# A two-head-group block on one core: latents' small rows inside the context's gate products, context decays behind the first scores, a head's end in the next head's stage

## The chip, the core and the metric

The kernel runs on one core of a Trainium2 chip. Five engines work side by side, each through its own list of instructions in order: PE (TensorE, matrix products; PEld is its weight load), DVE (VectorE, elementwise work and scans), ACT (ScalarE, functions and copies), POOL (GpSimd) and SP (SyncE, which here issues most DMAs). The metric is the time of one execution on the device in microseconds (us), the median over runs. The profile also shows the share of its clock that TensorE was granted, called PEclk or clock here.

## The reference

One layer of a hybrid block, for 512 latent tokens and 256 context tokens of width 2048. The two streams are normalised and modulated, projected with one weight matrix, run through four heads of gated linear attention (GLA) and four heads of mLSTM in both directions, gated, projected, and followed by a feed-forward block with a 3x3 convolution. What the change touches is the GLA and the gates of both groups:

```python
z = jnp.einsum('btd,dp->btp', h, w_in)
gq, gk, gv, gg, glr, mq, mk, mv, mo, mgate = jnp.split(z, PROJ_SPLITS, axis=-1)
dec = jnp.einsum('btr,zrk->zbtk', glr, gla_w_lr) + gla_b_lr[:, None, None, :]
gla_loga = jax.nn.log_sigmoid(dec) / GLA_NORMALIZER
# per chunk: S_t = diag(a_t) S_{t-1} + k_t v_t^T ; o_t = S_t^T q_t
# y_gla = rmsnorm(o) * silu(gate);   y_ml = sigmoid(ogate) * rmsnorm(h)
pre = mgate + mlstm_b_gate                    # input and forget gates of the mLSTM
```

`glr` (16 columns) and `mgate` (16 columns) are the small rows: they are needed before any decay or gate. The context is scanned first, and its last state starts the scan of the latents.

## The kernel before

All products are made from split operands (a high and a low part), three products for one, so that a block of 128 x 512 weights (`raw_h`, 512 KB) is loaded by DMA, its high part cast on ACT (`hi_h`), its low part subtracted on DVE (`lo_h`), and then used in 36 kinds of products named `a`.

The projection of one head (`project_steps`) takes 8 such blocks (`kp` 0 to 7), each in six steps (`a_0` to `a_5`). `weave` lays the chain of one head (a generator, its stage) into the projection of the next: the stage yields a number, and that many microseconds of projection products, by a table of costs, are put on PE before the stage goes on. On PE the written order is kept; on the other engines a list scheduler sets it. So the numbers that are yielded decide how much PE work covers each step's wait for ACT and DVE.

- Before the first stage, the small rows of latents and context are made as products `gm` (L592 to L598), with 32 columns each, four at a time; ACT copies them (`gm` copy), a product with a constant sums the four groups (`glr`, in `small_rows`, L601), ACT casts, DVE subtracts the low part.
- The first stage (`first_stages`) holds GLA heads 0 and 1, whose projections are done by then, and covers them with head 2's projection. `gla_prep` (L662) makes the decays of a head: `wlr` from a small weight (ACT cast L667, DVE L668), products `dec` for both directions, log-sigmoid (Abs, Exp, Ln on ACT, L641 to L643, then DVE L644), the context's products `cdec` and their log-sigmoid `cla`, the scans `bt` (L690), the context's sums `csum` and `kd` (L701).
- `gla` makes seven levels of scores: per level DVE subtracts decays twice (`ex`, L94), ACT takes two exponentials, DVE multiplies by q and k (L97), PE makes four products `sl`, DVE writes them under a mask (L762). Between them lie the states: `cst`, the transposes `ktt`, the products `st` with their update on DVE (L807), and at the end the outputs `po`. `finish` normalises a head (`ob`, L653), transposes it on PE (`yt`) and copies it (`yT`).
- The stage of head 3 ends with `ml_gates`: products `pre`, their bias on DVE (L842), a log-sigmoid, four scans, then transposes `pa` and products `pgc`. `mlstm` is the stage of each mLSTM head; its outputs `po` come in pairs of directions, with a reciprocal `dn` on DVE after each.
- `fill` works off fillers, one chunk of the modulation weights each (`raw_m`, 512 KB by DMA, one DVE operation of L320), at `rate` per weight block.

PE has two PSUM banks (`psb`) for all these small results, used in turn: a product waits until the result before last has been read.

Of the kernel before, what the change touches and what calls it, by code (L numbers as in the profile page):

```python
# [11 lines left out]
F32 = mybir.dt.float32  # L12
# [15 lines left out]
H = 4  # L28
# [55 lines left out]
def block_kernel(ctx: ExitStack, tc: tile.TileContext, a: dict, out: bass.AP):  # L84
# [318 lines left out]

    def project_first():

        banks = [acc(f"a0_{g}", BANKS[g]) for g in range(6)]
        both = accp.tile([P, CJ, T], F32, name="e0_c", tag="sums")
        sums = [None] * 4 + [both[:, j, 0 : DK + DV] for j in range(CJ)]
# [160 lines left out]
    nc.sync.dma_start(wsm, a["w_small"])  # L569
    cr = [tmp.tile([KT, P], F32, name=f"cr{i}", tag="rows") for i in range(2)]  # L570
# [15 lines left out]
    gm = [ytile(i, f"gm{i}", (P, n)) for i, n in enumerate((T, TC))]  # L586
    pinned[0] = True
    for c0, n, hs, m in ((0, T, hx, gm[0]), (T, TC, hc, gm[1])):
        ps = psb(f"gm{c0}", (P, n))
        for k in range(KT):  # L590
            g = 32 * (k % 4)
            parts = [h[k].bitcast(F32) for h in hs]  # L592
            if hs is hx and not 4 <= k < 8:
                parts = [xl[k]]
            for i, part in enumerate(parts):
                mm(ps[g : g + 32, :], wsm[:, k, :], part, start=(k < 4 and i == 0),
                   stop=(k >= 12 and i == len(parts) - 1), skip_group_check=True)
        S.copy(m, ps)  # L598
    st_0.close()

    def small_rows():  # L601
        for c0, n, m in ((0, T, gm[0]), (T, TC, gm[1])):
            ps = psb(f"glr{c0}", (96, n))
            mm(ps, cc(C_SA, 96), m, start=True, stop=True)
            o = glr[0:96, c0 : c0 + n]
            S.copy(o, ps)
            V.scalar_tensor_tensor(out=o, in0=o.bitcast(F32), scalar=cc(C_LO, 1, 96), in1=ps, op0=ALU.mult, op1=ALU.add)
            yield 1.4

# [52 lines left out]
    def gla_prep(h, out):  # L662

        raw = wtile(f"wlraw{h}", "wlraw", 2, DK)[0:98]
        nc.sync.dma_start(raw, a["w_lr"][h])
        wlr = wk.tile([98, 2, DK], F32R, name=f"wlr{h}", tag="wlr")
        S.copy(wlr, raw)  # L667
        V.scalar_tensor_tensor(out=wlr, in0=wlr.bitcast(F32), scalar=cc(C_LO + 1, 1, 98), in1=raw,  # L668
                               op0=ALU.mult, op1=ALU.add)
        la = wtile(f"la{h}", "la", 2, T)  # L670
        t = wtile(f"lt{h}", "tmp", 2, T)
        cla = wtile(f"cla{h}", "cla", CJ, 2, DK)
        ct = ytile(15, f"ct{h}", (P, CJ, 2, DK))
        for d in range(2):
            ps = psb(f"dec{h}{d}")
            mm(ps, wlr[:, d, :], glr[:, 0:T], start=True, stop=True)
            log_sigmoid(la[:, d], ps, t[:, d])
            yield
        ps = psb(f"cdec{h}", (P, CJ, 2, DK))
# [5 lines left out]
        bt = [ytile(8 + d, f"bt{h}{d}") for d in range(2)]  # L685
        for d in range(2):
            o, x = bt[d], la[:, d]
            if d == 1:
                o, x = o[:, ::-1], x[:, ::-1]
            V.tensor_tensor_scan(out=o, data0=cc(C_SEG, T), data1=x, initial=0.0, op0=ALU.mult, op1=ALU.add)  # L690
# [9 lines left out]
        kd = ytile(14, f"kd{h}", (P, 2, CJ, DK))  # L700
        S.activation(kd, ps, AF.Exp, scale=DECAY)  # L701
        ends = wtile(f"ends{h}", "ends", 2, 2, TJ - 1)
        for d in range(2):
            at = P * d + (P - 1) * (1 - d)
            V.tensor_scalar(out=ends[:, 0, d, :], in0=bt[d][:, at : at + 2 * P + 1 : P], scalar1=DECAY, scalar2=None,
                            op0=ALU.mult)
        S.activation(ends[:, 1], ends[:, 0], AF.Exp)
        out.update(bt=bt, kd=kd, ends=ends)
        yield

# [26 lines left out]
    def gla(h, pair, qk, v, kn, vn, yT, prep, fill, after, pending):  # L737
        bt, kd, ends = (prep[n] for n in ("bt", "kd", "ends"))
# [11 lines left out]
        yield fill[0]  # L750
        for lv, b in enumerate(LEVELS):
# [10 lines left out]
            V.copy_predicated(scd, msk[:, lv, :].unsqueeze(1).to_broadcast([P, TJ, P]), ps)  # L762
# [5 lines left out]
            if lv == 1:  # L768

                for j in range(CJ):  # L770
                    mul(kd[:, :, j], kd[:, :, j], kn[j].unsqueeze(1).to_broadcast([P, 2, DK]))
# [53 lines left out]
    def ml_gates():  # L825
# [11 lines left out]
        for t, r in ((0, li), (1, pf)):  # L837
            for c0, n, at in ((0, T, lat0), (T, TC, ctx0)):
# [5 lines left out]
                yield 1.4  # L844
        log_sigmoid(pf, pf, ab)
# [13 lines left out]
        yield 13  # L859
# [32 lines left out]
    def mlstm(h, _, qk, v, kn, vn, yT):  # L892
# [64 lines left out]
        for j in range(TJ):  # L957
            for d in range(2):
# [24 lines left out]
    def first_stages(tiles):  # L983

        yield from small_rows()
        prep = gla_prep(0, preps[0])
        for need in (0, 3, 3, 2.5):
            next(prep)
            yield need
        gla_ahead(0, preps[0])  # L990
        end = yield from gla(0, *tiles, yT, preps[0], (2, 1), gla_prep(1, preps[1]), lambda: None)
# [7 lines left out]
        gla_ahead(2, preps[2])  # L999

    def stages(h, tiles):

        yield 2.7
        if h >= H:
            yield from mlstm(h, *tiles, yT)
        elif h + 1 < H:
            end = yield from gla(h, *tiles, yT, preps[h], (4, 1.8), gla_prep(h + 1, preps[h + 1]), lambda: None)
            yield 5
            end()
            gla_ahead(h + 1, preps[h + 1])  # L1010
        else:
# [453 lines left out]
```

## Time and profile before

| | us |
|---|---|
| median of 3 runs | 2473.45 (2472.29 to 2475.78) |
| the profiled execution | 2479.69 |
| its span from first to last instruction | 2478.0 |
| PE busy | 2418.5 (98%) |
| DVE busy | 1792.9 (72%) |
| ACT busy | 1004.7 (41%) |
| mean granted clock | 0.992 |

The profiled execution is 6.24 us above the median; differences are taken within it. PE's share of busy time is high because the projections and the feed-forward part fill most of the span; the stages that the change touches lie between 197 us and 720 us, and what is lost there is seen only in a view of that stretch: PE's idle time, and the windows in which the granted clock is 0.50.

### The profile page before, as it was taken

To read this page: it belongs to the slowest core of one execution; us is meant where nothing else is said; L and a number is where in the kernel's file an instruction comes from. 1 tells how busy PE (TensorE), PEld (TensorE's weight loads), DVE (VectorE), ACT (ScalarE), POOL (GpSimd) and SP (SyncE) were. 2 spreads that over 40 slices of the span, in tenths; PEclk is the share of its full clock that TensorE was granted. 3 is DMA by queue.
4 is the path that set the end of the run, shared out by engine and by line. 5 is a ranking of instruction groups with operands and counts; after the bars stand their busy time and mean duration, and the time that the engine had idled before them with its cause. 6 is when DMAs were issued, how large, how long until landed. Compare 5 with 4: busy or idle time off the path is not lost.

```text
span 2478.0 us, 38665 instructions
## 1 busy us (share of the span) xinstructions
PE 2418.5 (98%) x15412; PEld 2179.5 (88%) x15412; DVE 1792.9 (72%) x2876; ACT 1004.7 (41%) x1494; POOL 177.4 (7%) x221
## 2 busy tenths in 40 slices
PE   6999989999999999999999999999999999999998
PEld 4887888889888888888999999999999999999997
DVE  6665855644457676669988787878687878787886
ACT  4224433222223232237544444444444444444445
POOL 0000000000000000000111111111101010101021
PEclk9999999999999999999999999999999999999999
DMA  9751111123345878853365555555546464646464
GB/s 383 277 178 49 45 43 43 61 82 113 128 163 190 265 269 306 271 184 115 97 168 125 148 123 147 124 144 124 141 120 152 120 152 117 156 115 158 119 181 135
DMA packets 122388, 373.65 MB, mean 151 GB/s; under 512 B 13912, under 2 KB 18912, under 8 KB 122208
## 3 DMA queue, kind: packets, MB, share of 16 engines
q1 hardware_dynamic: 95200, 318.75, 39.4%
q0 software_dynamic: 25920, 51.40, 11.5%
q8 instruction: 120, 1.97, 0.3%
q10 hardware_dynamic: 1088, 1.05, 0.1%
q14 instruction: 60, 0.49, 0.1%
HBM read 320.80 MB, written 50.34 MB: 150 GB/s over the span
## 4 chain that ended last, share of the span: by engine, by line
PE 81%; issue 10%; DVE 6%; DMA 1%; ACT 1%; POOL 1%; SPq 0%; DVEq 0%; POOLq 0%; ACTq 0%
PE a L111 18%; PE uv L111 16%; PE dn L111 15%; PE ug L111 15%; PE ga L111 7%; PE wo L111 3%; PE ps_m L111 2%; PE po L111 1%; PE sl L111 1%; DVE cv L1232 1%; DMA raw_uv<-in_w_up 1%; PE st L111 1%; PE cst L111 1%; DVE lo_d L106 0%; DVE ex L94 0%
## 5 line engine op out<-in xcount | busy, mean ns | idle before, releaser
L111 PE MATMUL dn<-gh,lo_d 128*128 128x512 f32 x672 | 263.0, 391 | 2.5 <-DVE lo_d L106 2.3
L111 PE MATMUL dn<-gh,hi_d 128*128 128x512 f32 x672 | 262.3, 390 | 0.0
L111 PE MATMUL dn<-gl,hi_d 128*128 128x512 f32 x672 | 262.1, 390 | 0.0
L1232 DVE SCALAR_TENSOR_TENSOR cv<-pads,cwt,cv 128x512 f32<-128x512 f32 x344 | 239.1, 746 | 0.6
L1286 POOL DMA_DIRECT2D x2d<-st x160 | 140.2, 932 | 1147.2 <-ACT st L1285 1069.0
L106 DVE TENSOR_TENSOR lo_buv<-sum_uv,hi_buv 128x1024 fp32r<-128x1024 f32 x80 | 98.0, 1225 | 102.5 <-ACT hi_buv L105 102.5
L320 DVE SCALAR_TENSOR_TENSOR raw_m<-raw_m,crow 128x1024 f32<-128x1024 f32 x128 | 152.8, 1219 | 2.6 <-DMA raw_m<-in_w_mod 2.6
L111 PEld LDWEIGHTS dn<-gh,lo_d 128*128 128x128 f32 x672 | 126.5, 188 | 31.4 <-DVE lo_d L106 5.3
L111 PE MATMUL a<-hi_h,hTh 128*128 128x256 f32 x512 | 149.7, 292 | 0.5 <-ACT e L402 0.5
L111 PEld LDWEIGHTS dn<-gl,hi_d 128*128 128x128 f32 x672 | 126.6, 188 | 26.1
L111 PEld LDWEIGHTS dn<-gh,hi_d 128*128 128x128 f32 x672 | 126.6, 188 | 25.8
L111 PE MATMUL a<-lo_h,hTh 128*128 128x256 f32 x512 | 145.3, 284 | 0.0
L111 PE MATMUL a<-hi_h,hTl 128*128 128x256 f32 x512 | 145.1, 283 | 0.0
L105 ACT CAST hi_d<-raw_d 128x1024 fp32r<-128x1024 f32 x86 | 88.7, 1031 | 131.6 <-PE ug L111 70.6
L106 DVE TENSOR_TENSOR lo_d<-raw_d,hi_d 128x1024 fp32r<-128x1024 f32 x86 | 102.9, 1196 | 48.8 <-ACT hi_d L105 48.1
L111 PE MATMUL ug<-bth,hi_bug 128*128 128x256 f32 x480 | 136.8, 285 | 0.1
L111 PE MATMUL uv<-bth,lo_buv 128*128 128x256 f32 x480 | 135.9, 283 | 0.8 <-DVE lo_buv L106 0.8
L111 PE MATMUL uv<-bqh,lo_auv 128*128 128x256 f32 x480 | 135.9, 283 | 0.0
L111 PE MATMUL uv<-bth,hi_buv 128*128 128x256 f32 x480 | 135.9, 283 | 0.0
L111 PE MATMUL ug<-bqh,lo_aug 128*128 128x256 f32 x480 | 135.8, 283 | 0.0
L111 PE MATMUL uv<-btl,hi_buv 128*128 128x256 f32 x480 | 135.8, 283 | 0.0
L111 PE MATMUL ug<-bqh,hi_aug 128*128 128x256 f32 x480 | 135.8, 283 | 0.0
(408 smaller groups left out, 7270.8 us busy)
## 6 DMA issues: line engine op xcount, KB each, us to landing
raw_m<-in_w_mod SPq DMA_DIRECT2D x192, 512.0 KB, 5.2
raw_d<-in_w_down SPq DMA_DIRECT2D x82, 512.0 KB, 3.5
raw_ug<-in_w_up SPq DMA_DIRECT2D x80, 512.0 KB, 3.5
x2d<-st POOLq DMA_DIRECT2D x160, 256.0 KB, 5.4
raw_uv<-in_w_up SPq DMA_DIRECT2D x80, 512.0 KB, 6.6
raw_h<-in_w_heads SPq DMA_DIRECT2D x64, 512.0 KB, 3.6
raw_ga<-in_w_gates SPq DMA_DIRECT2D x32, 512.0 KB, 4.2
raw_wo<-in_w_out SPq DMA_DIRECT2D x32, 512.0 KB, 4.4
```

The costliest lines, as they stand in the source:

```text
L105: cast[0] = S.copy(hi, x).ins
L106: return V.tensor_tensor(out=lo, in0=x, in1=hi.bitcast(F32), op=ALU.subtract).ins
L111: ins = PE.matmul(*args, **kw)
L320: V.scalar_tensor_tensor(out=x, in0=x, scalar=1.0, in1=crow[0], op0=ALU.mult, op1=ALU.mult, accum_out=mtot[:, at : at + 1])
L1232: V.scalar_tensor_tensor(out=t3, in0=src, scalar=w, in1=t3, op0=ALU.mult, op1=ALU.add)
L1286: nc.gpsimd.dma_start(x2d[k], t, accum_op=ALU.add)
```

## The change

1. The latents' `glr` product, with its copy and subtraction, is put behind the eighth k-tile of the context's `gm` products; the context's is put into the first stage, behind the second `dec`. The `gm` copies get high priority.
2. Head 0's small decay weight is loaded early into a spare part of another tile (`early_w`), ahead of the first stage.
3. In `gla_prep` of head 0 the scans come right behind the two `dec`, and the context's `cdec`, `csum` and `kd` are taken into `gla`, behind `sd` and behind the first scores (`first`). For other heads the scans come last, and the five steps of the preparation lie behind levels 2 to 6.
4. `finish` of GLA heads 0 to 2 is run behind the first scores of the next head; of head 3 it is run in `ml_gates`, behind the four `pre`.
5. The yielded numbers are others: 1.75 and 0.85 in the first stage (2 and 1, 2.1 and 1.1 before), 4.1 and 2 (4 and 1.8), 2.7 and 1.3 (2.8 and 1.2), 15.6 for the gates' scans (13), and in `mlstm` 2 per direction (1.4 or 2.7 per pair).
6. Fillers come at 1.25 per weight block in all of a head's blocks, before at 2 in the last five; both make ten per head.

```diff
@@ project_steps
-            rate[0] = 2 if h > H and kp >= 3 else 0
+            rate[0] = 1.25 if h > H else 0
@@ the small rows
+    early_w = early_both[0][0:98, :, DK + DV :]
+    nc.sync.dma_start(early_w, a["w_lr"][0])
...
+    def small_rows(i):
+        c0, n = ((0, T), (T, TC))[i]
+        ps = psb(f"glr{c0}", (96, n))
+        mm(ps, cc(C_SA, 96), gm[i], start=True, stop=True)
+        o = glr[0:96, c0 : c0 + n]
+        with tc.high_priority():
+            S.copy(o, ps)
+            V.scalar_tensor_tensor(out=o, in0=o.bitcast(F32), scalar=cc(C_LO, 1, 96), in1=ps, op0=ALU.mult, op1=ALU.add)
...
-        S.copy(m, ps)
+            if c0 and k == 7:
+                small_rows(0)
+        with tc.high_priority():
+            S.copy(m, ps)
@@ gla_prep
+        if h == 0:
+            scans()
+            yield
         ps = psb(f"cdec{h}", (P, CJ, 2, DK))
...
+        out["kd"] = ytile(14, f"kd{h}", (P, 2, CJ, DK))
+        S.activation(out["kd"], ps, AF.Exp, scale=DECAY)
         yield
+        if h:
+            scans()
+            yield
@@ gla
         yield fill[0]
+        if next(first, 1) is None:
+            yield fill[1]
...
+            yield fill[0]
             if lv == 0:
+                next(first, 1)
                 pending()
-            yield fill[0]
-            if lv in (2, 3, 4, 6) and next(after, 1) is None:
+                yield fill[1]
+            if lv > 1 and next(after, 1) is None:
                 yield fill[1]
@@ ml_gates
+        end()
+        yield 1.4
         log_sigmoid(pf, pf, ab)
...
-        yield 13
+        yield 15.6
@@ mlstm, behind each direction of an output
+                yield 2
             S.activation(junk, ob[:, j, :], AF.Square, accum_out=ssq[:, j : j + 1])
-            yield 1.4 if h < 2 * H - 1 else 2.7
@@ first_stages
-        yield from small_rows()
         prep = gla_prep(0, preps[0])
-        for need in (0, 3, 3, 2.5):
-            next(prep)
-            yield need
+        next(prep)
+        yield 1
+        next(prep)
+        yield 1.4
+        small_rows(1)
+        yield 1.4
+        next(prep)
+        yield 2.8
         gla_ahead(0, preps[0])
-        end = yield from gla(0, *tiles, yT, preps[0], (2, 1), gla_prep(1, preps[1]), lambda: None)
+        end = yield from gla(0, *tiles, yT, preps[0], (1.75, 0.85), gla_prep(1, preps[1]), lambda: None, prep)
...
-        end = yield from gla(1, *tiles, yT, preps[1], (2.1, 1.1), gla_prep(2, preps[2]), end)
-        yield 4
-        end()
+        end = yield from gla(1, *tiles, yT, preps[1], (1.75, 0.85), gla_prep(2, preps[2]), end)
         gla_ahead(2, preps[2])
+        ends.append(end)
@@ stages
-            end = yield from gla(h, *tiles, yT, preps[h], (4, 1.8), gla_prep(h + 1, preps[h + 1]), lambda: None)
-            yield 5
-            end()
+            end = yield from gla(h, *tiles, yT, preps[h], (4.1, 2), gla_prep(h + 1, preps[h + 1]), ends.pop())
...
-            end = yield from gla(h, *tiles, yT, preps[h], (2.8, 1.2), iter(()), lambda: None)
-            yield 5
-            end()
-            yield from ml_gates()
+            end = yield from gla(h, *tiles, yT, preps[h], (2.7, 1.3), iter(()), ends.pop())
+            yield from ml_gates(end)
```

What the scheduler makes of it is seen in the engines' own lists. First ACT, at the end of the `gm` products, before (`gm0` and `gm1` are latents' and context's rows, `glr0` and `glr512` their sums, `dec00` the first product with the decay weight `wlr0`):

```order
L598 COPY gm0_1966<-gm0_1968 128x512
L598 COPY gm1_1967<-gm512_1990 128x256
L606 CAST glr_92<-glr0_2054 96x512
L667 CAST wlr0_2094<-wlraw0_2092 98x256
L606 CAST glr_92<-glr512_2076 96x256
L641 ACTIVATE lt0_2098<-dec00_2101 128x512
```

And ACT at the same place now:

```order
L616 COPY gm0_1967<-gm0_1969 128x512
L599 CAST glr_92<-glr0_2008 96x512
L616 COPY gm1_1968<-gm512_1991 128x256
L676 CAST wlr0_2059<-e0_c_184 98x256
L649 ACTIVATE lt0_2063<-dec00_2066 128x512
```

The latents' cast has moved ahead of the context's copy, and the cast of `wlr0` still stands behind that copy, which waits for the last `gm` product; on PE `dec00` now follows the last `gm` product with nothing between.

Second DVE, at the end of head 0, from the mask of its last level (`sl0_6`) to its last state (`st02`), before (`ex1` are head 1's decays, `kd1` its context's weights):

```order
L762 COPY_PREDICATED sc0_2201<-msk_60,sl0_6_2501 128x512
L94 TENSOR_TENSOR ex1_0_2605<-bt11_2532 128x256x2
L94 TENSOR_TENSOR ex1_1_2610<-bt10_2531 128x128x2x2
L94 TENSOR_TENSOR ex1_1_2610<-bt11_2532 128x128x2x2
L97 TENSOR_TENSOR ex1_0_2605<-ex1_0_2605,e4_0_1259 128x512
L97 TENSOR_TENSOR ex1_0_2605<-ex1_0_2605,e4_1_1268 128x512
L97 TENSOR_TENSOR ex1_1_2610<-ex1_1_2610,e4_0_1259 128x512
L97 TENSOR_TENSOR ex1_1_2610<-ex1_1_2610,e4_1_1268 128x512
L97 TENSOR_TENSOR kd1_2542<-kd1_2542,e0_c_184 128x2x128
L807 SCALAR_TENSOR_TENSOR st02_2548<-st01_2489,ends0_2169,st02_2549 128x256 x2
```

And DVE there now (`lo_h2_5` is the low part of a weight block of head 2):

```order
L780 COPY_PREDICATED sc0_2148<-msk_60,sl0_6_2479 128x512
L94 TENSOR_TENSOR ex1_1_2573<-bt10_2497 128x128x2x2
L97 TENSOR_TENSOR ex1_0_2568<-ex1_0_2568,e4_0_1259 128x512
L94 TENSOR_TENSOR ex1_1_2573<-bt11_2498 128x128x2x2
L97 TENSOR_TENSOR ex1_0_2568<-ex1_0_2568,e4_1_1268 128x512
L106 TENSOR_TENSOR lo_h2_5_2657<-raw_h2_5_2654,hi_h2_5_2656 128x1024
L828 SCALAR_TENSOR_TENSOR st02_2517<-st01_2467,ends0_2116,st02_2518 128x256 x2
```

Five operations of head 1 and of the weights stand between mask and state, eight before. On PE the six products `csum` and 24 products `a` stood between `sl0_6` and `st02` before; now it is 18 products `a`.

Third DVE, at the end of head 3 (`ob3`, normalised in L653, now L661) and the start of the gates (`pre`), before:

```order
L821 COPY ob3_4123<-po3_3_4154 128x256
L173 TENSOR_SCALAR var3_4196<-ssq3_4121 128x4
L175 SCALAR_TENSOR_TENSOR scr3_4197<-rs3_4198 128x4
L97 TENSOR_TENSOR scr3_4197<-scr3_4197,var3_4196 128x4
L177 SCALAR_TENSOR_TENSOR rs3_4198<-scr3_4197,rs3_4198 128x4
L653 TENSOR_SCALAR ob3_4123<-ob3_4123,rs3_4198 128x256 x4
L106 TENSOR_TENSOR lo_h4_6_4301<-raw_h4_6_4298,hi_h4_6_4300 128x1024
L842 TENSOR_SCALAR li_4223<-pre00_4230,bg_100 4x512 x2
L842 TENSOR_SCALAR li_4223<-pre0512_4240,bg_100 4x256 x2
```

And now:

```order
L842 COPY ob3_4122<-po3_3_4165 128x256
L863 TENSOR_SCALAR li_4171<-pre00_4178,bg_100 4x512
L863 TENSOR_SCALAR li_4171<-pre0512_4188,bg_100 4x256 x2
L863 TENSOR_SCALAR pf_4172<-pre10_4198,bg_100 4x512 x2
L106 TENSOR_TENSOR lo_h4_6_4300<-raw_h4_6_4297,hi_h4_6_4299 128x1024
L863 TENSOR_SCALAR pf_4172<-pre1512_4214,bg_100 4x256 x2
L173 TENSOR_SCALAR var3_4224<-ssq3_4120 128x4
L175 SCALAR_TENSOR_TENSOR scr3_4225<-rs3_4226 128x4
L97 TENSOR_TENSOR scr3_4225<-scr3_4225,var3_4224 128x4
L177 SCALAR_TENSOR_TENSOR rs3_4226<-scr3_4225,rs3_4226 128x4
L661 TENSOR_SCALAR ob3_4122<-ob3_4122,rs3_4226 128x256 x4
```

The normalisation stood ahead of the four `pre` and now stands behind them and a weight block. On PE the transposes `yt` of head 3 had 30 products `a` between them and the last `po`; now they follow the four `pre` with 24 products `a` among and behind these. The transposes `pa` have 84 products `a` ahead of them, 120 now.

More of the change, by code (lines that the diff above doesn't have):

```diff
@@ L678, in gla_prep, with scans @@
             yield
+        def scans():
+            bt = [ytile(8 + d, f"bt{h}{d}") for d in range(2)]
+            for d in range(2):
+                o, x = bt[d], la[:, d]
+                if d == 1:
+                    o, x = o[:, ::-1], x[:, ::-1]
+                V.tensor_tensor_scan(out=o, data0=cc(C_SEG, T), data1=x, initial=0.0, op0=ALU.mult, op1=ALU.add)
+            ends = wtile(f"ends{h}", "ends", 2, 2, TJ - 1)
+            for d in range(2):
+                at = P * d + (P - 1) * (1 - d)
+                V.tensor_scalar(out=ends[:, 0, d, :], in0=bt[d][:, at : at + 2 * P + 1 : P], scalar1=DECAY, scalar2=None,
+                                op0=ALU.mult)
+            S.activation(ends[:, 1], ends[:, 0], AF.Exp)
+            out.update(bt=bt, ends=ends)
+        if h == 0:
+            scans()
+            yield
         ps = psb(f"cdec{h}", (P, CJ, 2, DK))
@@ L699, in gla_prep @@
                     mm(ps[:, d, j, :], ones, cla[:, 1 - j, d, :], start=False, stop=True)
[L700 to L708, printed above, removed]
+        out["kd"] = ytile(14, f"kd{h}", (P, 2, CJ, DK))
+        S.activation(out["kd"], ps, AF.Exp, scale=DECAY)
         yield
+        if h:
+            scans()
+            yield
     def crossed(ex, b, fwd):
@@ L735, in gla_ahead, with gla @@
         prep["ex"] = [level_decays(h, lv, prep["bt"]) for lv in range(2)]
[L737 to L738 removed]
+    def gla(h, pair, qk, v, kn, vn, yT, prep, fill, after, pending, first=iter(())):
+        bt, ends = prep["bt"], prep["ends"]
         sc = wtile(f"sc{h}", "sc", 2, TJ, P)
```

25 lines of the change are left out of this document (8 added, 17 removed).

## The prediction

> **What bounds the kernel now.** I read the head of the page first, then the busy time of PE in stretches, then PE's waits, and only then single steps.
>
> ```profile
> span 2478.0 us, 38665 instructions
> PE 2418.5 (98%) x15412; PEld 2179.5 (88%) x15412; DVE 1792.9 (72%) x2876; ACT 1004.7 (41%) x1494; POOL 177.4 (7%) x221
> ```
>
> PE is the bound, at 98% of the span, so what the change can give is only what PE loses where the change is. The next view gives PE alone by stretch: from and to, length, busy time with the number of instructions, granted clock, DMA share, GB/s. The first five stretches are the first stage (heads 0 and 1), head 2, head 3's end with the gates, the mLSTM stages in two parts; the last four are the pieces of them in which the clock was halved.
>
> ```profile
> 200.00:330.00 130.00, 115.69 (x705) 0.96 0.13 40
> 330.00:416.00 86.00, 84.38 (x525) 0.98 0.14 44
> 462.00:512.00 50.00, 46.80 (x279) 0.90 0.19 64
> 512.00:720.00 208.00, 203.51 (x1212) 1.00 0.36 115
> 720.00:1100.00 380.00, 380.00 (x1727) 1.00 0.74 251
> 217.20:220.60 3.40, 3.40 (x13) 0.50 0.35 130
> 323.01:329.84 6.83, 5.30 (x16) 0.50 0.00 0
> 411.76:415.17 3.41, 3.41 (x11) 0.50 0.00 0
> 493.68:503.92 10.24, 8.40 (x37) 0.50 0.15 51
> ```
>
> Length less busy time is what PE stands idle: 14.31, 1.62, 3.20 and 4.49 us, and nothing from 720 on. Work done at half the clock takes twice its time, so half of the busy time there is lost as well: 1.70 and 2.65 in the first stage, 1.70 in head 2, 4.20 at the gates. I call the four stretches A, B, C and D. They lose A 14.31 + 4.35 = 18.66, B 3.32, C 7.40, D 4.49, together 33.9 us. That is the ceiling of any gain. Who is waited for stands in PE's waits between 200 and 720 us (total, times, longest):
>
> ```profile
> PE yt L116 <- DVE ob L653: 6.5, 2, 4.9
> PE po L111 <- DVE dn L966: 4.0, 3, 1.3
> PE csum L111 <- DVE cla L644: 3.2, 1, 3.2
> PE pgc L111 <- DVE dg L878: 2.0, 1, 2.0
> PE csum L111 <- DVE st L807: 1.7, 1, 1.7
> PE sl L111 <- DVE cla L644: 1.3, 1, 1.3
> PE pa L116 <- DVE cum L100: 0.9, 1, 0.9
> PE po L111 <- DVE st L807: 0.8, 1, 0.8
> PE yt L116 <- DVE sc L762: 0.4, 1, 0.4
> ...
> 409.91 1.55 PE L116 MATMUL yt<-cst,ob 128*128 128x128 f32 x8 [1.62 <-DVE ob L653]
> ```
>
> All are waits for DVE. The first row holds 4.9 us at the end of A and the 1.62 us of B, whose own row is the last one: 1.85 us behind that gap's end the clock is halved for 3.41 us.
>
> **The change part by part: the first stage (A).** These are the durations (ACT and PE as single instructions, DVE as groups of the stage with total and mean ns):
>
> ```profile
> 200.80 0.37 ACT L598 COPY gm<-gm 128x256 f32<-128x256 f32 x1 [2.90 <-PE gm L111]
> 203.38 0.41 ACT L667 CAST wlr<-wlraw 98x256 fp32r<-98x256 f32 x1 [0.98 <-DMA wlraw<-in_w_lr]
> ...
> 200.06 0.69 PE L111 MATMUL gm<-hcl,wsm 128*32 128x256 f32 x8
> 200.68 1.10 PE L111 MATMUL glr<-gm,cst 128*96 128x512 f32 x2
> 201.84 0.39 PE L111 MATMUL a<-hTl,hi_h 128*128 128x512 f32 x1
> 202.07 0.40 PE L111 MATMUL a<-hTh,lo_h 128*128 128x512 f32 x1
> ...
> L668 DVE SCALAR_TENSOR_TENSOR wlr<-wlr,cst,wlraw 98x256 fp32r<-98x256 f32 x4 | 1.9, 476 | 0.7 <-ACT wlr L667 0.7
> L690 DVE TENSOR_TENSOR_SCAN bt<-cst,la 128x512 f32<-128x512 f32 x6 | 7.1, 1212 | 0.0
> L94 DVE TENSOR_TENSOR ex<-bt 128x512 f32<-128x512 f32 x32 | 23.2, 758 | 0.2
> L97 DVE TENSOR_TENSOR ex<-ex,qk 128x1024 f32<-128x1024 f32 x9 | 10.9, 1216 | 1.8 <-ACT ex L730 1.8
> L762 DVE COPY_PREDICATED sc<-msk,sl 128x512 f32<-128x512 uint8 x14 | 10.3, 738 | 2.7 <-PE sl L111 2.7
> L106 DVE TENSOR_TENSOR lo_h<-raw_h,hi_h 128x1024 fp32r<-128x1024 f32 x8 | 9.7, 1216 | 2.5 <-ACT hi_h L105 2.5
> L97 DVE TENSOR_TENSOR ex<-ex,e 128x512 f32<-128x512 f32 x14 | 9.2, 687 | 3.8 <-ACT ex L729 2.3 <-ACT ex L730 1.5
> L644 DVE SCALAR_TENSOR_TENSOR la<-dec,lt 128x512 f32<-128x512 f32 x6 | 4.0, 687 | 5.8 <-ACT lt L643 5.8
> ```
>
> *What goes.* The wait of `csum` for `cla` (3.2 us, and the halved clock behind it), that for `st` (1.7) and that of `yt` (4.9, and two half windows) lose their causes: `csum` no longer stands ahead of the first scores' chain, and head 1's `finish` is issued behind head 2's first scores. That a wait goes isn't a gain yet; I therefore count all of A's 18.66 as removed, and then put in what is late in the new order.
>
> *What is late next,* five places.
> - `dec00` directly follows the last `gm`. It needs `wlr`, whose cast stands behind the context's `gm` copy on ACT: copy 0.37, cast 0.41, DVE's low part 0.48, and three handings-over; 1.4 us. PE's queue holds nothing else meanwhile. Bounds 0.8 (the scheduler's ACT gets past the copy early) and 2.0.
> - `sl_0` of head 0. DVE must get through, from `la` on: two L644 (1.4), two scans (2.4), four L94 (3.0), the subtractions of `glr` (0.5 by L668's row), the product for `kt` and that for `sc` (1.4 as two of 0.69), then `qi`, a `lo_h` and `ex`·`qk`, three of 1.22 (3.7): 12.4 us, about 0.5 less because neighbours overlap. Ahead of it are three functions on ACT of some 0.6 each with their handings-over (about 2.3), together 14.2. PE on its side has `dec`, 60 products `a` and `glr`, `sd`, `cdec` till there, 12.3 us by 0.23 a product of 512 columns (two starts of the rows above) and half of that for 256. 14.2 − 12.3 = 1.9 us. Bounds 0.3 and 3.1, as the scheduler's order on DVE is tight or not.
> - `po_0` of head 0 needs `st02`. DVE has between the mask of `sl0_6` and it, by the order shown: mask 0.74, two L94 1.52, two L97 of 512 1.37, a `lo_h` 1.22, `st` 0.47: 5.3 us and 0.2 of handing-over (L762's 2.7 us of waits over 14). PE has 18 products there, 3.5 us. Wait 2.0; bounds 0.5 and 3.1. Since a 1.62 us gap was followed by a half window in B, I add one: 1.7.
> - `yt` of head 0 keeps its place behind the first scores of head 1, but the fill falls from 2.1 to 1.75: 0.4 + 0.35, 0.7 us.
> - `po_0` of head 1: 0.8 + 0.35, 1.2 us.
>
> That leaves 1.4 + 1.9 + 2.0 + 0.7 + 1.2 = 7.2, and 1.7 of clock: 8.9. **A gains 18.66 − 8.9 = 9.8.** The `glr` product cuts the row of `gm` products in two; it started 0.62 us behind the last `gm` where `a` products follow each other in 0.23. I take 0.3 us for this, between nothing and 0.6. The early DMA of `wlr` is one issue of SP moved ahead, not added; it costs nothing while SP only waits for buffers.
>
> [...]
>
> **Head 2's end (B).** `finish` of head 2 now runs behind head 3's first scores. The normalisation on DVE and ACT gets the whole of `gla_ahead`, `sd` and one level as cover, 4 us of fill and more where 1.62 us was missing. **B gains 3.3**; bounds 1.6 (a wait as long at another place, no half window) and 3.3.
>
> **The gates (C).**
>
> ```profile
> L842 DVE TENSOR_SCALAR pf<-pre,bg 4x512 f32<-4x512 f32 (+1 forms) x4 | 2.4, 609 | 0.7 <-PE pre L111 0.7
> L653 DVE TENSOR_SCALAR ob<-ob,rs 128x256 f32<-128x256 f32 x4 | 1.1, 348 | 0.0
> ```
>
> The scans now get 15.6 + 1.4 = 17 us of fill against 13; `pa` and `pgc` missed 0.9 + 2.0 = 2.9, so both waits go. But the end of head 3 is taken behind the `pre`, and DVE does it late: from the first `li` to the last `ob` it has eight L842 (`li` as `pf`, 4.9), a `lo_h` (1.2), four small ones (0.6) and four L653 (1.4), 8.1 us, against 24 products `a` of 0.23 = 5.6 on PE: `yt` waits 2.5, with a half window behind it (1.7). The second `pre` waits for its bank, 0.4. I keep one of the three half windows at `pa` (1.7), since small products with steps of DVE among them stay there. Left: 6.3. **C gains 7.4 − 6.3 = 1.1**; bounds −3 (all three windows stay beside the new wait) and +5.
>
> **mLSTM (D).**
>
> ```profile
> L320 DVE SCALAR_TENSOR_TENSOR raw_m<-raw_m,crow 128x1024 f32<-128x1024 f32 x128 | 152.8, 1219 | 2.6 <-DMA raw_m<-in_w_mod 2.6
> ...
> raw_m<-in_w_mod SPq DMA_DIRECT2D x192, 512.0 KB, 5.2
> ```
>
> Before, 1.4 us lay between pairs, and a `lo_h` and a chunk of modulation (1.22 each) got in between DVE's steps for `dn`: 1.3 us missing three times. Now two yields of 2 us lie between a product and the next in its bank, 4 us against 2.4 for those two and the small steps of `dn`. **D gains 4.3** of 4.49; bounds 2 (a second chunk, 1.22, gets in at two of three heads) and 4.5. Fillers stay ten per head, and spread from five weight blocks to eight; by the last two rows a chunk is loaded in 5.2 us, and in 128 of them DVE waited for its chunk 2.6 us in all. POOL's order stays, and SP issues the same DMAs, those of `raw_m` earlier.
>
> **Sum:** 9.8 + 3.3 + 1.1 + 4.3 − 0.3 = 18.2. The profiled execution took 2479.69 us, 6.24 above the median; 2479.7 − 18.2 = 2461.5, and at the level of the median 2455.3: **2455 us**.
>
> **Rivals.**
> - *DVE is the bound of the first stage.* The same work of DVE then only shows up at other waits. For it: every wait of A ends on DVE. Against it: the last 4.9 and the first 3.2 were waits on a chain, not on a full engine. A would gain 1 instead of 9.8: 2464 (2460 to 2470).
> - *Slower: chunks in mLSTM's line.* Fillers now begin with the first weight block of a head, where `qs`, states and `dn` stand in DVE's line. If the 512 KB of a chunk are issued too late, DVE stands on it, and PE behind. Three such chunks in each of three heads, each missing 5.2 − 2.4 (its landing less two DVE operations ahead of it) = 2.8, make 25 us: 2480. It decides once a chunk is issued less than 5.2 us before its turn; the 2.6 us of waits in 128 chunks speak against it.
> - *All new waits but `dec00` covered.* By the low ends of my bounds: 7.5 less in A (5.8 of waits, 1.7 of clock), 5.9 less in C: 18.2 + 13.4 = 31.6, 2442.
> - *The clock doesn't fall behind gaps as short as these.* 1.7 in A and 3.4 in C stay out: 2450. For it: 1.3 us gaps in D left the clock of D at 1.00; against it B's row. [...]
>
> **How the numbers follow.** Forecast 0.44, DVE as bound 0.20, slower by chunks 0.12, all covered 0.10, no fall of the clock 0.14. The range 2442 to 2469 leaves out the slower case and the worst of the second. About 0.2% (5 us) is what can be told from no change here: faster, below 2468.5, are the forecast, the two better cases and three quarters of DVE's, 0.83; the last quarter is within it, 0.05; slower 0.12.
>
> **What the profile of the changed kernel would show.** Right: no rows `csum<-cla`, `pgc<-dg` and `po<-dn` among PE's waits, no `yt` of 4.9; new ones for `dec` (1.4, on `wlr`), `po` on `st` (2.0) and `yt` near the gates (2.5); the stretch of head 2 busy throughout at clock 1.00, as is the mLSTM part. Wrong: PE idle as long in A with other names in the rows; DVE's L320 with 10 us or more of waits for `raw_m`; half windows in places where I have none, above all behind `dec00`, or none at all.

## The result, and the profile after

The changed kernel took 2451.73 us in the median of 4 runs (2448.89 to 2453.94), the kernel before 2473.68 beside it (2472.29 to 2475.78): ratio 0.991, 95% interval 0.9893 to 0.9927. That is 22.0 us less; 18 were forecast. A second group of runs gave 2451.70 against 2474.23, ratio 0.991 (0.9896 to 0.9923).

The profiled execution took 2453.06 us, its span 2451.2; 26.6 less than the profiled one of before, which lay 6.24 above its median. How much of this is from the changed stretch is seen between two PE instructions outside it, the first `gm` and the first `ga`, the product that follows the last mLSTM stage. The first two rows are of before, the next two of the changed kernel (start, us):

```profile
192.73 0.64 PE L111 MATMUL gm<-xl,wsm 128*32 128x512 f32 x4
739.31 0.40 PE L111 MATMUL ga<-hTh,hi_ga 128*128 128x512 f32 x1
```

```profile
192.47 0.64 PE L111 MATMUL gm<-xl,wsm 128*32 128x512 f32 x4
717.33 0.40 PE L111 MATMUL ga<-hTh,hi_ga 128*128 128x512 f32 x1
```

546.58 us before, 524.86 now: 21.7 us. Nearly all of the other 4.9 of this pair of executions lies behind `ga` (1738.7 us before, 1733.9 now). There the execution of before had three windows of 3.41 us at half clock, from 1104.67 and from 1742.96 us on, and the one of the changed kernel a single one, from 1083.90 us on, which makes 3.4 us; another 1.1 us is idle time. The medians lie 22.0 apart, so I don't count this as a gain of the change.

PE by stretch, of the changed kernel, with the stretches moved to about the same work (the last two rows are the only pieces at half clock in them):

```profile
197.00:327.00 130.00, 123.14 (x805) 0.99 0.13 42
327.00:412.00 85.00, 85.00 (x542) 1.00 0.17 51
455.00:505.00 50.00, 47.61 (x295) 0.97 0.30 95
505.00:712.00 207.00, 206.84 (x1240) 1.00 0.38 123
257.87:261.28 3.41, 3.40 (x8) 0.50 0.51 154
462.67:466.08 3.41, 3.41 (x16) 0.50 0.17 67
```

And PE's waits between 190 and 720 us, all of them:

```profile
PE po L111 <- DVE st L828: 3.2, 3, 2.1
PE yt L116 <- DVE ob L661: 2.2, 1, 2.2
PE sl L111 <- DVE ex L97: 1.7, 1, 1.7
PE dec L111 <- DVE wlr L677: 1.3, 1, 1.3
PE sl L111 <- ACT ktt L818: 0.7, 1, 0.7
PE sl L111 <- DVE sc L828: 0.4, 1, 0.4
PE pre L111 <- DVE ob L842: 0.2, 1, 0.2
```

The rows `csum`, `pgc`, `pa`, `po<-dn` and the 4.9 us of `yt` are gone. The four longest new waits (2.2, 2.1, 1.7 and 1.3) are those that were costed; `sl` on `ktt` and on `sc` were not. Lost to PE by idle time and halved clock, counted as in the prediction, which takes half of the busy time at half clock as lost, 1.70 of 3.41 us (products `a` of 512 columns start 0.43 us apart there, 412.83 to 414.53 us of before, and 0.23 apart at full clock, 415.30 to 416.45, which would make it 1.6):

| stretch | before | forecast to be left | measured left |
|---|---|---|---|
| A, first stage | 18.66 | 8.9 | 6.86 + 1.70 = 8.6 |
| B, head 2's end | 3.32 | 0 | 0 |
| C, gates | 7.40 | 6.3 | 2.39 + 1.70 = 4.1 |
| D, mLSTM | 4.49 | 0.2 | 0.16 |

The table gives 33.9 − 12.9 = 21.0, to which head 3 (412 to 455) adds a new wait of 0.5 for `st`; 20.5 of the 21.7. The last 1.2 us are neither idle time nor half clock in the profile; the mLSTM's yields, further down, show where such time can come from.

### The profile page after: what moved, and what is told of

It reads as the page before. It is cut to its first block, busy times and chain, and to the rows that moved or that the text cites. A ratio compares the mean times of both kernels' runs of the same rounds, so it can differ in the third digit from the quotient of the medians.

```text
span 2451.2 us, 38648 instructions
## 1 busy us (share of the span) xinstructions
PE 2406.2 (98%) x15412; PEld 2170.5 (89%) x15412; DVE 1795.0 (73%) x2876; ACT 1003.7 (41%) x1494; POOL 176.5 (7%) x221
## 4 chain that ended last, share of the span: by engine, by line
PE 88%; issue 6%; DVE 3%; DMA 2%; ACT 1%; POOL 0%; SPq 0%; DVEq 0%; POOLq 0%; ACTq 0%
PE a L111 19%; PE dn L111 17%; PE uv L111 16%; PE ug L111 15%; PE ga L111 7%; PE wo L111 7%; PE po L111 2%; PE ps_m L111 1%; PE sl L111 1%; DMA raw_m<-in_w_mod 1%; PE st L111 1%; PE cst L111 1%; DMA raw_uv<-in_w_up 0%; DVE ex L94 0%; DMA xl<-in_xT 0%
## 5 line engine op out<-in xcount | busy, mean ns | idle before, releaser
L111 PE MATMUL uv<-bql,hi_auv 128*128 128x256 f32 x480 | 135.8, 283 | 0.0
```

What stands on the lines that cost most here:

```text
L111: ins = PE.matmul(*args, **kw)
```

## Experiments

Each kernel below is the changed one with one edit, run 4 to 6 times beside the kernel before on the same chip; in brackets stand the ratio and its 95% interval. The changed kernel itself stood at −22.0 and −22.5 us against before; the differences below are to be read beside that, with intervals of 3 to 4 us to each side. PE's waits in the traces are far sharper, since in a second execution of the changed kernel they came back to 0.1 us. Sharper too is the stretch from the first `gm` to the first `ga` in the profiled executions, 524.86 and 523.23 us as changed, of which the clock cost 3.4 and 1.7 us. Not undone by themselves were the early load of `wlr`, the priority of the `gm` copies and the yields of the first stage.

**The ends of heads 1 to 3 in their own stages again (e1).** Head 0's end stood behind head 1's first scores before the change too, and stays there.

```diff
+        yield 4
+        end()
         gla_ahead(2, preps[2])
-        ends.append(end)
...
-            end = yield from gla(h, *tiles, yT, preps[h], (4.1, 2), gla_prep(h + 1, preps[h + 1]), ends.pop())
+            end = yield from gla(h, *tiles, yT, preps[h], (4.1, 2), gla_prep(h + 1, preps[h + 1]), lambda: None)
+            yield 5
+            end()
...
-            yield from ml_gates(end)
+            yield 5
+            end()
+            yield from ml_gates()
```

> The changed kernel with the ends of heads 1, 2 and 3 run again in their own stages (4 or 5 us of products ahead of each), all else as changed. Theory, that each wait is a chain with too little cover: the waits of yt for ob come back, about 4.9 us at the end of the first stage and 1.6 at the end of head 2, with three half-clock windows (4.35 us), and the 2.2 us with its half window (1.7) at the gates goes: 4.9 + 1.6 + 4.35 - 3.9 = 7.0 us more than 2451.7, 2458.7. Rival, that DVE's amount of work bounds these stages and a wait taken away comes back elsewhere: within 2 us of 2451.7.

Measured 2467.30 against 2474.20, −6.9 (0.9971, 0.9959 to 0.9982): 15 us of the gain are lost, twice what was expected. In the profiled executions the stretch from `gm` to `ga` is 14.5 us longer than in the first of the changed kernel, 9.8 of it idle time and 4.9 lost to the clock. PE's waits there have this row at their head, and its longer wait is this one in the timeline:

```profile
PE yt L116 <- DVE ob L661: 9.2, 2, 5.3
```

```profile
411.35 0.48 PE L116 MATMUL yt<-cst,ob 128*128 128x128 f32 x1 [5.28 <-DVE ob L661]
```

The rival falls: without the moved ends the waits are there, and the time is far more than 2 us longer. But head 2's is 5.3 us, not 1.6, and in the trace no product `a` stands between its last `po` and its `yt`. My suspicion was that the yields of 4.1 and 2 (4 and 1.8 before) now spend head 2's products earlier, which only a head without an end of its own can afford. The next kernel tests that.

**The same, with the yields of heads 2, 3 and the gates as before too (e6).**

```diff
-            end = yield from gla(h, *tiles, yT, preps[h], (4.1, 2), ...
+            end = yield from gla(h, *tiles, yT, preps[h], (4, 1.8), ...
...
-            end = yield from gla(h, *tiles, yT, preps[h], (2.7, 1.3), ...
+            end = yield from gla(h, *tiles, yT, preps[h], (2.8, 1.2), ...
...
-        yield 15.6
+        yield 13
```

> As e1_ends_back, and with the yields of heads 2, 3 and the gates as before the change too (4 and 1.8, 2.8 and 1.2, 13). Theory, that in e1 the raised yields had used up head 2's products before its end: the wait of yt there falls from 5.3 to 1.6 us, and the gates wait 0.9 and 2.0 as before; 13 us more than 2451.7 in all, about 2464.5. Rival, that the end itself takes longer in the new order: 5.3 us stay, 2467 as in e1.

Measured 2464.86 against 2473.42, −8.6 (0.9967, 0.9954 to 0.9979). Head 2's transposes in the timeline, and then the gates in PE's waits:

```profile
404.81 0.33 PE L116 MATMUL yt<-cst,ob 128*128 128x128 f32 x1 [1.20 <-DVE ob L661]
406.60 0.59 PE L116 MATMUL yt<-cst,ob 128*128 128x128 f32 x2 [1.46 <-DVE ob L661]
```

```profile
PE pgc L111 <- DVE dg L899: 1.8, 1, 1.8
PE pa L116 <- DVE cum L100: 1.0, 1, 1.0
```

Head 2's wait falls to 1.2 + 1.5 us (1.6 was expected) and the gates wait as before: the products had been spent. By the medians about 14 us of the gain come from the moved ends with the yields that belong to them, by the stretch from `gm` to `ga` (534.38 us) 9.5 to 11.2. Without the ends, the yields of heads 2, 3 and the gates are worth nothing or less: the two medians, 2.4 us apart, can't be told apart, but the stretch is 5.0 us longer in e1.

**mLSTM: the yields back alone (e2), and the fillers back alone (e3).**

```diff
-                yield 2
             S.activation(junk, ob[:, j, :], AF.Square, accum_out=ssq[:, j : j + 1])
+            yield 1.4 if h < 2 * H - 1 else 2.7
```

> The changed kernel with the mLSTM's outputs covered as before (1.4 us behind each pair, 2.7 in the last head), fillers spread over all weight blocks as changed. Theory, that the two yields of 2 us cover dn: three waits of po for dn of about 1.3 us come back, 4 us more, 2455.7. Rival, that the spreading of the fillers took the modulation chunks out of DVE's way there: no such waits, 2451.7.

```diff
-            rate[0] = 1.25 if h > H else 0
+            rate[0] = 2 if h > H and kp >= 3 else 0
```

> The changed kernel with fillers again at 2 per weight block in the last five blocks of a head, the mLSTM's yields of 2 us as changed. Theory: two yields are cover enough for a chunk of 1.22 us, no wait of po for dn above 0.3 us, 2451.7 (0 to 1 us more). Rival, that the spreading brought the gain: waits of 1.3 us come back, 2455.7.

With the yields back: 2455.60 against 2474.20, −18.6 (0.9921, 0.9907 to 0.9934). With the fillers back: 2453.96, −20.2 (0.9919, 0.9905 to 0.9932). The only row of PE's waits between 505 and 720 us in the first, against none in the second:

```profile
PE po L111 <- DVE dn L987: 1.1, 3, 0.4
```

Both theories had a part of it. By the waits, spreading the fillers took 4.0 us down to 1.1, and the yields of 2 us cover them even with the fillers as before; either would have taken away most of them. By time the yields are worth more: e2's median is at the theory's 2455.7, though not by the theory's waits, and its interval still overlaps that of the changed kernel. Its stretch from `gm` to `ga` is 527.67 us (e3: 525.05), 2.8 more than the longer one of the changed kernel with the same loss to the clock, and only 1.5 of that is idle time. The rest fits PE's start behind a wait: in the profile of before, the `po` at 543.57 us with 1.32 us of idle time ahead of it starts 1.70 us behind the start of the product before it, where 0.22 is usual, so 0.16 us are lost beside the idle time. My estimate from this for e2's six such places (three of 0.37 us, three of 0.12) is 1.0 us. It may be what lacks in the sum of the whole change as well, with 20 places above 0.1 us before and 9 now.

**Head 0's context decays ahead of its first scores again (e4).**

```diff
-        if h == 0:
-            scans()
-            yield
         ps = psb(f"cdec{h}", (P, CJ, 2, DK))
...
-        next(prep)
-        yield 2.8
+        for need in (2.6, 2.7, 0):
+            next(prep)
+            yield need
```

> The changed kernel with head 0's context decays (cdec, csum, kd) again ahead of the scans and of the first scores. Theory: csum waits for cla about 3 us with a half-clock window behind it (1.7), and the 1.7 us of the first scores' wait goes: 3 us more, 2454.7. Rival, that DVE's amount of work bounds the first stage: the wait only changes its name, within 1 us of 2451.7.

Measured 2456.55 against 2474.20, −17.7 (0.9928, 0.9915 to 0.994), 4 to 5 us worse than as changed; all its five runs (2455.57 to 2460.29) lie above all eight of the changed kernel (2448.89 to 2453.94). From PE's waits:

```profile
PE csum L111 <- DVE cla L652: 2.0, 1, 2.0
PE sl L111 <- DVE cla L652: 1.8, 1, 1.8
PE sl L111 <- ACT ktt L814: 1.7, 1, 1.7
```

The wait of `csum` is back with 2.0 us, not 3, and without a half window, so the loss isn't made up as the theory said; more comes from the scores of both heads that then wait at three places. PE's idle time in 190 to 720 us is 13.8 us, 9.9 as changed. The rival, that the wait only changes its name, falls by these 3.9 us.

**The latents' small rows behind the `gm` products again (e5).**

```diff
-            if c0 and k == 7:
-                small_rows(0)
...
+        small_rows(0)
+        yield 1.4
+        small_rows(1)
+        yield 1.4
         prep = gla_prep(0, preps[0])
...
-        yield 1.4
-        small_rows(1)
```

> The changed kernel with the latents' small rows no longer inside the context's gm products: both glr products stand again ahead of head 0's decays, 1.4 us of products behind each. Theory, that this part of the change buys 2.8 us of products for later at the price of dec's 1.3 us: dec's wait goes, the first scores' wait stays at 1.7, and the end of the first stage, with 2.8 of some 4 us of products fewer, waits up to 2 us: within 2 us of 2451.7. Rival, that the chain of head 0 is what this part shortens: 3 us more or above.

Measured 2457.88 against 2473.42, −15.5 (0.9934, 0.9921 to 0.9948): 6 to 7 us worse, all five runs (2455.5 to 2459.93) above all eight of the changed kernel, so my theory falls and the rival holds. PE's longest waits:

```profile
PE sl L111 <- DVE ex L97: 4.5, 1, 4.5
PE yt L116 <- DVE ob L659: 3.6, 2, 2.2
PE po L111 <- DVE st L826: 2.5, 3, 1.4
```

Where `dec` starts, here and then in the changed kernel (first `gm` at 192.33 and 192.47 us):

```profile
205.84 0.62 PE L111 MATMUL dec<-glr,wlr 98*128 98x512 f32 x2
```

```profile
203.02 0.50 PE L111 MATMUL dec<-glr,wlr 98*128 98x512 f32 x1 [1.33 <-DVE wlr L677]
```

`dec` no longer waits, but it starts 3.0 us later behind the first `gm`, and the first scores wait 4.5 us instead of 1.7. From `dec` to these scores the chain through ACT and DVE takes about as long as in the changed kernel (14.0 us, 14.5 there), but PE has 9.5 us of work beside it instead of 12.8: 24 products `a` now stand ahead of `dec`, and 12 fewer behind it, where the chain runs.

**Head 0's decay weight split earlier (m1).** Its cast and low part go into a free `y` tile ahead of the `gm` products.

```diff
+    early_wlr = ytile(14, "wlr0", (98, 2, DK), F32R)
+    split_wlr(early_wlr, early_w)
...
-        wlr = wk.tile([98, 2, DK], F32R, name=f"wlr{h}", tag="wlr")
-        S.copy(wlr, raw)
...
+        wlr = early_wlr if h == 0 else wk.tile([98, 2, DK], F32R, name=f"wlr{h}", tag="wlr")
+        if h:
+            split_wlr(wlr, raw)
```

> The changed kernel, with head 0's decay weight split into a tile of its own (a free part of the y tiles) ahead of the gm products, so that its cast no longer stands behind the context's gm copy. Theory, that dec waits for this cast alone: its 1.3 us go and nothing takes their place, 1.3 less. Rival, that dec then waits for the rest of its chain (glr's low part): 0 to 0.5 less.

It was run beside the changed kernel itself, for which was written:

> The changed kernel again, as the measure for the next three on the same chip. 2451.7 by its first runs. PE's gaps (dec 1.3, first sl 1.7, po of head 0 2.0, yt at the gates 2.2) come back to 0.1 us, since every engine's order is fixed; the windows of halved clock may lie elsewhere, if they follow a grid of 3.41 us that starts anew in each execution.

The changed kernel gave 2451.70 against 2474.23, with all its gaps back within 0.1 us; this one 2452.84 (0.9914, 0.9901 to 0.9928): no difference that can be told. `dec` doesn't wait any more, and only 0.2 us of it came back at the first scores (1.9 for 1.7), as PE's waits show:

```profile
PE sl L111 <- DVE ex L97: 1.9, 1, 1.9
```

So the cast was what `dec` waited for. That 1.1 us less of idle time don't show in the median may be the work of the clock, told further down: against the first profile of the changed kernel, with the same loss to the clock (3.4 us), the stretch from `gm` to `ga` is 1.0 us shorter (523.88).

**More products behind head 0's last state (m2).**

```diff
-                yield fill[1]
+                yield fill[1] + (2 if h == 0 and n == 2 else 0)
```

> The changed kernel, with 2 us more of products of head 2 behind head 0's last state, taken from the 24 that are left at the end of the first stage. Theory, that po of head 0 waits 2.0 us for a state that stands behind five steps of DVE: the wait goes to under 0.3 and, where that gap had halved the clock, 1.7 more, 2 to 3.7 less. Rival, that DVE is full: the wait goes on to the next steps of head 0 and 1, under 1 less.

Measured 2451.48 against 2474.23 (0.9909, 0.9896 to 0.9923): the same as the changed kernel. The 2.0 us of `po` for `st` are gone, and in their place PE's waits have:

```profile
PE yt L116 <- DVE ob L661: 2.9, 2, 2.2
PE sl L111 <- ACT ktt L818: 2.0, 2, 1.3
...
PE sd L111 <- DVE sc L97: 0.8, 1, 0.8
PE sl L111 <- DVE cla L652: 0.8, 1, 0.8
```

PE's idle time is 10.3 us, for 9.95 beside it. Here the rival holds: the 2 us go on to head 0's `yt`, to `ktt`, to `sd` and to the next scores.

**Head 3's normalisation ahead of the `pre` (m3).** `finish` is split in two, its DVE part first, its transposes where they were.

```diff
+            next(end)
             yield from ml_gates(end)
...
-        end()
+        next(end)
```

> The changed kernel, with head 3's end split: its normalisation on DVE ahead of the four pre, its transposes behind them as in the changed kernel. Theory, that yt waits 2.2 us only because DVE has the pre's steps and a weight block first: the wait and its half window (1.7) go, up to 0.5 comes back at the pre, 3.4 less. Rival, that the pre then wait for the normalisation: 2 us of waits at the pre, 0 to 1.7 less.

Measured 2454.83 against 2474.23 (0.9917, 0.9904 to 0.9931), no better. In the timeline the wait has another name:

```profile
461.70 0.63 PE L116 MATMUL yt<-cst,ob 128*128 128x128 f32 x4 [1.64 <-DVE pf L866]
462.70 0.63 PE L116 MATMUL yt<-cst,ob 128*128 128x128 f32 x4 [0.37 <-DVE pf L866]
```

Neither reading was right: the normalisation was done at 460.05 us, but `yt` takes the two banks that the `pre` use, and DVE read the last two `pre` (`pf`) only then, up to 461.56 and 462.55 us. Both steps are in DVE's line; which goes first matters little.

**Cover moved to where it is missing (m5, m8).** The early split, 1.8 us more products ahead of the first scores, and 2.4 us ahead of head 3's transposes, first out of the gates' 15.6 us, then out of what follows the gates.

```diff
-        yield 2.8
+        yield 4.6
         gla_ahead(0, preps[0])
...
+        yield 2.4
         end()
...
-        yield 15.6
+        yield 13.2
```

> The changed kernel with the early split of head 0's decay weight (m1), 1.8 us more of products ahead of the first scores, and 2.4 us of the gates' 15.6 us laid ahead of head 3's transposes. Theory, that these three waits are chains with too little cover and there are products to spare: dec 1.3, sl 1.7 and yt 2.2 us go, and the gates' half window (1.7) with them: 5 to 7 less, 2445 to 2447. Rival, that DVE is full in the first stage, as m2 had it: only the gates' part comes, 2448, and the gaps of head 0 turn up under other names.

> As m5_cover_moved, but with the gates' 15.6 us of products kept behind head 3's transposes, so that the 2.4 us ahead of them come out of those that follow the gates. Theory, that pgc waits 1.2 us in m5 for the 2.4 us taken from it: its wait falls under 0.5 us, and the half windows there (3.2) with it: 2446 (2444 to 2448). Rival, that the wait goes on to the first mLSTM head, which has six products fewer: its waits for DVE grow by about 1 us, 2448 to 2450.

(The last kernel is without the line of 13.2.) Both took 2449.63, against 2473.42 (0.990, 0.9886 to 0.9913) and 2474.41 (0.990, 0.9884 to 0.9917), −23.8 and −24.8. PE's idle time between 190 and 720 us fell from 9.9 to 6.6 us in both; the time fell by 2 us, within the uncertainty, so neither is shown to beat the changed kernel by its median, and both miss their theories' 2445 to 2447 and 2446. By the stretch from `gm` to `ga` (520.63 and 519.04 us) they are 2.6 to 5.8 us shorter. The waits for `yt` at the gates are gone, and of head 0's some stay under other names. At the gates one wait takes the place of another, in the first kernel `pgc` for `dg`, in the second `pa` for `gcol`, of which I had not thought (the rival's wait in the first mLSTM head isn't there). The first from PE's waits, the second from the timeline:

```profile
PE pgc L111 <- DVE dg L910: 1.2, 1, 1.2
```

```profile
481.13 0.34 PE L116 MATMUL pa<-cst,li 4*128 4x4 f32 x3 [1.68 <-DVE gcol L914]
```

## Why the prediction was right

The forecast was 2455, measured 2451.7, within the range and faster as said. The number alone would fit the rival with no fall of the clock (2450) better; the trace, with half windows behind two of the new gaps in the first profile and behind one in the second, lies between them. Taken by its steps:

- *What goes, and the ceiling of 33.9 us:* right. The rows named as going all went, and 21.7 of the 33.9 us came.
- *`dec00`, 1.4 us:* measured 1.3, and the early split shows that the cast behind ACT's copy was the cause.
- *First scores, 1.9 us:* measured 1.7, and both sides of the count hold: from the first `dec` to the scores the chain takes 14.5 us (14.2 counted), PE's work 12.8 (12.3).
- *State of head 0, 2.0 us:* measured 2.05, by luck. Two terms were left out and made up for each other: DVE came to the mask 1.75 us after the scores were done (at 251.04), and PE had four products `st` and two `po` (1.5 us) behind the 18 `a`. From the scores' end to the state it is 6.8 us, not 5.5, against 4.8 of PE's work, not 3.5. The half window behind it is luck too: it is there in this execution and not in the second, where A loses 6.9 us instead of 8.6. DVE's mask and state in the timeline:

```profile
252.79 0.73 DVE L780 COPY_PREDICATED sc<-msk,sl 128x512 f32<-128x512 uint8 x1
256.96 0.86 DVE L828 SCALAR_TENSOR_TENSOR st<-st,ends,st 128x256 f32<-128x256 f32 x2
```

- *`yt` of head 0, 0.7, and `po` of head 1, 1.2:* too high; nothing and 0.6. These two were carried over from before with an addition for the smaller fill. In their place stood `sl` on `ktt` (0.7) and `sl` on `sc` (0.4), which I hadn't listed. A's sum came out at 8.6 for 8.9 because these made up for each other, which is luck.
- *The row of `gm` products cut by `glr`, 0.3 us:* about right, from a row read wrongly. The 0.62 us was counted from the start of the last eight `gm` products; `glr` starts 0.31 us behind the start of the last one. Between the first `gm` and the end of the last there lie 8.02 us before and 9.23 now. Most of these 1.2 us is `glr`'s own time, moved here: where it stands behind the `gm` products (e5), it holds up the products behind it by about 0.9 us. Some 0.3 is left.
- *B, 3.3, and D, 4.3:* right, both. For D the reason was half of it: the yields alone cover all of it (e3), but the fillers' spreading alone takes away 2.9 of the 4.0 us too (e2).
- *C, gain 1.1:* the term that was mis-sized. `yt` waits 2.2 for 2.5, with its half window, since it needs only the first of the four `ob` (it starts at 462.57 us, and DVE is at the four from 462.07 to 463.21); the second `pre` waits 0.2 for 0.4, and the half window kept at `pa` isn't there: the clock between 470 and 490 us is 1.00. 4.1 are left instead of 6.3. That is 2.2 of the 3.3 us by which the forecast was too high. The half window was kept because small products stay there, but the waits among them, 0.9 and 2.0 us before, are gone.

Of the rivals, *DVE as the bound of the first stage* falls as a whole, since the change and three undone parts moved PE's idle time there by microseconds. But it holds for what is left: m2 took 2 us away at one place and found them at four others. *No fall of the clock behind short gaps* is, in the first profile, true for two of the new gaps (`dec` 1.3, first scores 1.7) and wrong for two (`po` 2.05, `yt` 2.2); the last section tells more. *Chunks in mLSTM's line* didn't come: DVE waits for no chunk there. *All new waits but `dec00` covered* didn't come either; it was also priced below the low ends it names, as it takes the first scores and `po` at nothing, not 0.3 and 0.5, and C's gain above its bound of 5.

What the parts are worth, each by its undoing, by the medians and then by the stretch from `gm` to `ga` in the profiled executions: the ends with their yields 14 and 9.5 to 11.2, the small rows 6 to 7 and 5.2 to 6.8, the context's decays 4 to 5 and 3.0 to 4.7, the mLSTM's yields 3 to 4 and 2.8 to 4.4, its fillers alone 2 and 0.2 to 1.8, which can't be told from none. By the medians that is more than 22 together; that the parts of the first stage share the same products would explain it, but no run undoes two of those at once.

## What to carry to other kernels

Where one engine is the bound and the others run in chains beside it, count for each wait what stands ahead of it in the other engine's line, by durations from the trace, and set against it the bound engine's own work up to that place; this came out to 0.3 us at the three largest new waits here, at one of them by luck, since what the other engine is still busy with when the chain reaches it belongs to the count as well. Cover is a stock: work that is given to one wait is missing at a later one, so a larger yield pays only with the move that frees it (head 2's `yt` waits 5.3 us in e1 and 1.2 + 1.5 in e6), and cover spent ahead of a chain's first step is wasted (in e5 `dec` starts 3.0 us later and the first scores wait 4.5 us for 1.7). Look also at what a product needs beside its operands: a bank that is still to be read delays it as a late operand does (`yt` in m3, by 1.64 and 0.37 us).

## What the clock did

In each of the two profiles the distances between the halved pieces of the clock are whole multiples of 3.413 us. In that of before the pieces start at 217.20, 323.01, 411.76 and 493.68 us (3.41, 6.83, 3.41 and 10.24 us long), and the last three lie 31, 57 and 81 times 3.413 us behind the first. In that of the changed kernel they start at 257.87, 462.67 and 1083.90 us, the last two 60 and 242 times 3.413 us behind the first. What is called a window below is a stretch of this length, counted from a halved piece of the same execution.

Unexpected was that one gap was followed by different clocks. The wait of `po` in head 0 is 2.05 us in both of the following executions of the same program. In the first it lies whole in one window (busy 1.37 of 3.41), which ends where the wait does, and the next window is at 0.50:

```profile
254.46:257.87 3.41, 1.37 (x7) 1.00 0.00 0
257.87:261.28 3.41, 3.40 (x8) 0.50 0.51 154
```

In the second, with the windows counted from its half window at 460.46, one ends 1.64 us ahead of the wait's end (257.30). The gap falls on two windows (0.41 and 1.64 us idle), and the clock stays at 1.00:

```profile
252.25:255.66 3.41, 3.00 (x14) 1.00 0.11 29
255.66:259.07 3.41, 1.77 (x8) 1.00 0.44 138
259.07:262.48 3.41, 3.41 (x17) 1.00 0.04 16
```

In two other kernels PE stands idle in one window for 1.80 us (the kernel with the context first), with no fall behind it, and for 1.92 us (the early split), with one:

```profile
210.18:213.59 3.41, 1.61 (x11) 1.00 0.00 0
213.59:217.00 3.41, 3.25 (x22) 1.00 0.00 0
```

```profile
212.68:216.09 3.41, 1.49 (x9) 1.00 0.19 44
216.09:219.50 3.41, 3.41 (x19) 0.50 0.28 112
```

What decides between the two isn't shown. At other places the clock fell behind less idle time: behind 1.56 us in B of before (408.35 to 411.76 us, with eight transposes `yt`), from which I had taken the half windows of the prediction, and behind 1.02 us at the gates of before (490.27 to 493.68 us, with ten `pa`). Behind 1.32 us in D of before, with `po` and products `a`, it stayed at 1.00, three times (windows from 541.47, 619.97 and 698.48 us on). And in 497.09 to 500.51 us of before (`a`, `pa` and `pgc`), itself at 0.50, PE isn't idle at all, and the next window is at 0.50 again.

So the same gap of 2.05 us had a halved window behind it, 1.7 us as counted above, in one execution and none in the other. That may be why runs of one kernel differ by 1.6 to 8 us, and why the early split shows no gain: its 1.92 us lay whole in a window. No run moves a gap of one length against the windows and changes nothing else, so all this is read from traces and not shown by an experiment.
